# A one-core hybrid S5 and attention layer: where the side steps of the input projection stand

## The chip, the cores and the metric

The program runs on one core of a Trainium2 chip. The metric is the device time in microseconds (us). Three runs of the kernel before took 1403.91, 1406.46 and 1409.44 us; the median is 1406.46 us.

## The reference, cut to what matters

One layer works on 2048 prompt rows and 64 sample rows of width 1024. The rows are normalised and modulated, and go through one input projection with 3080 columns. Its results are split into the S5 input `u`, two gates `z`, the attention operands `q`, `k`, `v`, and eight forget logits per row.

```python
h = _rmsnorm(x, norm_g) * (1.0 + scale[:, None, :]) + shift[:, None, :]
proj = h @ w_in
u, z_s, q, k, v, z_a, f_logit = jnp.split(proj, IN_SPLITS, axis=-1)
y_ssm, h_re, h_im = _s5_segment(u, ...)        # 32 groups, 64 complex states each, a scan over time
...
logf = jax.nn.log_sigmoid((f_logit + b_f).astype(f32))
cum = jnp.cumsum(logf, axis=1)                 # the bias of the attention scores
...
y = x + gate[:, None, :] * (jnp.concatenate([y_ssm, y_att], axis=-1) @ w_out)
```

## The kernel before, in words

The program has four stages: norms of the first half of the rows, the input projection, a gated unit (GLU) with attention, and the output projection. Only the projection stage is touched by the change.

**The projection.** `InProj.line` (line 654) goes through a list of stretches. A stretch is one piece of 128 to 264 columns of `w_in` against two of the four row groups `g` (512 rows each, 576 in the last), and a stretch is cut into blocks. A block is one accumulation in one PSUM bank over the eight pieces `k` of the inner dimension, as three products per `k` (`whi` with both parts of `h`, `wlo` with the high part), 24 products in all. Each block is a generator that yields four times, every two `k`. The last two blocks of a stretch are interleaved, so that the buffers of their weights come free one after the other. Three PSUM banks (`low`) go round among the blocks; TensorE can start a block only when the bank's last content has been read out: by a copy `ev` on ScalarE for `k`, `v` and `q` (line 637), by a tanh `th` on ScalarE (L354 is the line of the helper) and a product on VectorE (L608) for `z`. The weights of the next stretch come by DMA into `wst`, ScalarE casts a high part `whi` (L319), and VectorE subtracts to `wlo` (L323).

**The side steps.** Everything else of this stage is one long generator, `side`, made by `rest()` (line 2054): the norms of the other half of the rows, the S5 set-up, 16 S5 sets, parts of the operands of the output projection, the forget logarithms, the bias of the attention and the start of the GLU. `line` takes steps from it by a share: after each block it adds the block's size times the stretch's rate (1 for `k` and `q`, 2 for `v`, 1.5 for `z`, up to 4 for `u`) to `share`, and takes that many steps (lines 688 to 691). So all of a block's steps stand behind the block's last product. TensorE's own order is the order of the program text, pinned by `Chain`. On VectorE, ScalarE and the SyncE queue (SP) a scheduler chooses the order when the program is built.

**An S5 set** (two groups of 16 channels). `consts` (line 961) builds the set's matrices in seven steps; its fifth transposes `btt` on TensorE, ScalarE copies the result to `bt` (L1010), and TensorE makes `kd` from `ca` and `bp`. `run` (line 1044) multiplies `us` by `bt` on TensorE in its first step, and then scans. `outs` (line 1102) makes the set's outputs with `tm` and `ca`. `sets` (line 1120) interleaves the steps of a set (`r`) with those of the next set's matrices (`o`):

```python
for x in "ro", "o", "r", "o", "o", "r", "o":     # line 1147: seven steps; the last "o" is the fifth of consts
    for y in x:
        next({"r": r, "o": o}[y], None)
    yield
```

The next step of `side` begins with `run` of the next set, whose product needs `bt`.

**The forget logarithms.** `logf` (line 698) stands in `rest()` behind the last S5 set. It switches ScalarE's function table (`table`, line 331), takes Abs, Exp and Ln of the logits `lf` into `lab`, finishes `lf` on VectorE (L708), switches the table back, stores `lf` to the output (L710, L711), loads it again in another order of rows (L713, L717), gives six empty steps (line 718), and then makes cumulative sums on TensorE with `triu` and `ones`. The logits of the last rows are made by the stretch `k` 1536 over the row groups 0 and 1, the fifteenth of the 24 stretches.

Of the kernel before, what the change touches and what calls it, by code (L numbers as in the profile page):

```python
# [17 lines left out]
P = 128  # L18
# [10 lines left out]
H = 8  # L29
# [419 lines left out]
class InProj:  # L449


    def __init__(self, e):
        self.e = e

        self.ht = Region(e.nc)
        self.hs = ([0, 512], [36, 512]), ([16, 640], [52, 576])
        self.dec = Region(e.nc, (70, 72), bufs=1)
        self.wp = Region(e.nc, R_WP)
        self.xp = Region(e.nc, R_X, (R_S5U[1] - 4, R_S5U[1]))
        self.ev = Region(e.nc, R_EV, bufs=2)  # L460
        self.wlo = e.V
        self.ps = Banks(e.psum, 2, 3, 4)
        self.h = {}
        self.normed = {}

    def tiles(self, g):

# [186 lines left out]
    def line(self, stretches, side, ready=None):  # L654


        w = ready
        if not w:
            w = self.fetch(*self.columns(*stretches[0][:2]))
            for _ in range(4):  # L660
                self.part(w)
        share = 0
        for j, (kind, base, row, gs, rate, after) in enumerate(stretches):
            nw = None
            bs = list(self.blocks(kind, row, gs, w))
            at = 0
            more = j + 1 < len(stretches)
            while at < len(bs):

                now = bs[at:at + (2 if more and at == len(bs) - 2 else 1)]  # L670
                for _ in range(KT // 2):
                    for _, _, b in now:
                        next(b)
                if at == 0 and more:
                    nw = self.fetch(*self.columns(*stretches[j + 1][:2]))
                at += len(now)
                with self.e.tc.high_priority():
                    if nw and at == 3:
                        self.part(nw)
                    if nw and at == len(bs):  # L680
                        while len(nw.hi) < KT:
                            self.part(nw)
                    for _, _, b in now:
                        next(b, None)
                g = now[-1][1]
                if after and (at == len(bs) or bs[at][1] != g):
                    after(g)
                share += sum(size for size, _, _ in now) * (rate[g] if isinstance(rate, dict) else rate)
                while share >= 1:
                    share -= 1  # L690
                    next(side, None)
                with self.e.tc.high_priority():
                    for _, _, b in now:
                        for _ in b:
                            pass
            w = nw

    def logf(self, ps):

        e = self.e  # L700
        nc, V, S, PL, PE = e.nc, e.V, e.S, e.PL, e.PE
        sb = self.ev
        lf = e.lf
        ab = sb.tile([P, 17, H], F32, tag="lab", name="lab", bufs=1)
        S.activation(ab, lf, AF.Abs)
        e.act(ab, ab, AF.Exp, scale=-1.0)
        e.act(ab, ab, AF.Ln, bias=1.0)
        V.scalar_tensor_tensor(lf, lf, 0.0, ab, op0=ALU.min, op1=ALU.subtract)  # L708
        lf_p, lf_s = e.o["lf_p"][0, 0], e.o["lf_s"][0, 0]
        nc.sync.dma_start(lf_p.rearrange("(f p t) h -> p f (t h)", f=2, t=TC), lf[:, :16].rearrange("p (f t) h -> p f (t h)", f=2))  # L710
        nc.sync.dma_start(e.rows(lf_s, 16), lf[:DEC, 16])  # L711

        nc.sync.dma_start(lf[:, :16], lf_p.rearrange("(t p) h -> p t h", p=P))  # L713
        cl = sb.tile([P, 5, H], F32, tag="cl", name="cl", bufs=1)
        V.memset(cl, 0.0)
        nc.sync.dma_start(cl[:, :4], e.clf.rearrange("(t p) h -> p t h", p=P))
        nc.sync.dma_start(cl[:DEC, 4], lf_s)  # L717
        for _ in range(6):
            yield
        for src, n, c0 in ((lf, 16, 0), (cl, 5, 16)):  # L720
            yield
            w = n * H
            sv = src[:, :n].rearrange("p t h -> p (t h)")
            pc = ps.tile([P, 512], F32, name="pc")
            PE.matmul(pc[:, :w], e.triu, sv, start=True, stop=True)
            pt = ps.tile([P, 512], F32, name="pt")
            PE.matmul(pt[:, :w], e.ones, sv, start=True, stop=True)
            off = sb.tile([P, 16, H], F32, tag="off", name="off", bufs=1)
            V.memset(off[:, 0], 0.0)
            yield  # L730
            for t in range(1, n):
                if t == 8:
                    yield
                V.tensor_tensor(off[:, t], off[:, t - 1], pt[:, (t - 1) * H:t * H], op=ALU.add)
            V.scalar_tensor_tensor(e.cm.rearrange("p h t -> p t h")[:, c0:c0 + n], off[:, :n], -1.0,
                                   pc[:, :w].rearrange("p (t h) -> p t h", h=H), op0=ALU.mult, op1=ALU.subtract)


class S5:
# [380 lines left out]
    def sets(self):  # L1120

        self.k, self.f = {}, {}
        self.load(0)
        o = self.consts(0)
        for _ in range(5):
            next(o)
            yield
        for s in range(NSET + 1):
            if s < NSET:
                r = self.run(s)  # L1130
                if s + 1 < NSET:
                    self.load(s + 1)
                next(r)
            if s:
                self.outs(s - 1)

            next(o, None)
            yield
            if s == NSET:
                break  # L1140
            next(r)
            next(o, None)
            yield
            next(r)
            yield
            o = self.consts(s + 1) if s + 1 < NSET else iter(())
            for x in "ro", "o", "r", "o", "o", "r", "o":
                for y in x:
                    next({"r": r, "o": o}[y], None)
                yield  # L1150
# [838 lines left out]
def body(tc, a, o):  # L1989
    with ExitStack() as top:  # L1990
# [63 lines left out]
        def rest():  # L2054
# [2 lines left out]
            yield from s5_setup  # L2057
            c = 0
            for n, _ in enumerate(s5.sets()):
                if n % 18 == 6 and c < 9:  # L2060
                    if c < 8:
                        out.raw_operands(c)
# [4 lines left out]
            assert c == 9  # L2067
            yield from s5.final()
            yield
            e.table("natural_log_exp_and_others", AF.Tanh, AF.Gelu_apprx_tanh)  # L2070
            yield from ip.logf(s5.ps)
            e.table("gelu_apprx_tanh_and_others", AF.Exp, AF.Ln, AF.Abs)
            made.append(Attn(e))
            yield
            yield from made[0].bias(s5.ps)
# [7 lines left out]
        for half in ((2, 3), (0, 1)):  # L2083
            for i, (kind, base, row) in enumerate(ip.PARTS):
                after = (lambda g: ip.get(g - 2)) if half[0] and i == 9 else None
                ts.append((kind, base, row, half, {"v": 2, "z": 1.5}.get(kind, 1), after))
        ip.line(ts, side, w)
        n = 0
# [46 lines left out]
```

## Time and profile before

| What | us |
|---|---|
| Median of the runs (lowest, highest) | 1406.46 (1403.91, 1409.44) |
| Span of the profiled execution (the page gives no other time for it) | 1410.9 |
| TensorE (PE) busy | 1318.9 |
| VectorE (DVE) busy | 972.3 |
| ScalarE (ACT) busy | 655.9 |
| GpSimd (POOL) busy | 519.8 |
| End of the projection's products, start of the GLU's | 742.9, 744.2 |

The profiled execution has a span 4.4 us above the median of the runs, and 1.5 us above the slowest of them.

In the rows below, a time stands first in microseconds from the start of the span. Of a group of instructions the page gives the line, engine, operation, what is written and read, the count, the busy time, and the idle time of the engine before them with what ended it. "PEclk" is the share of full clock that TensorE was granted. L154 is the helper line of every matrix product, L157 that of every transpose, L323 and L329 helpers of VectorE and GpSimd, so the names of the tiles tell what an instruction is.

### The profile page before, as it was taken

What the parts mean: (1) busy time and instruction counts of PE and PEld (TensorE: products, weight loads), DVE (VectorE), ACT (ScalarE), POOL (GpSimd) and SP (SyncE); (2) the same over time, 40 slices, a digit from 0 to 9 for tenths busy, and PEclk for the clock granted to TensorE, in tenths of its full rate; (3) what the DMA queues carried; (4) which work ended last, traced back from release to release, by engine and by line L of the source; (5) the groups of instructions that cost most, each with busy time, mean ns of one, the idle gap of its engine ahead of it and who ended that gap; (6) DMA issues with size and microseconds to landing.
All of it is one profiled execution on the core that took longest, in us unless ns stands there. A gap on an engine that the chain in (4) does not pass through costs nothing.

```text
span 1410.9 us, 25901 instructions
## 1 busy us (share of the span) xinstructions
PE 1318.9 (93%) x9164; PEld 1036.0 (73%) x9164; DVE 972.3 (69%) x2404; ACT 655.9 (46%) x1710; POOL 519.8 (37%) x502
## 2 busy tenths in 40 slices
PE   5898999999999899999899899999999999798998
PEld 2787999998888889898688755555555555387887
DVE  3635896987786679764326968786787786355775
ACT  3645365567443575574214435544544545522221
POOL 1100254566443446352004113423323325733453
PEclk9998999999999999999999979999999999999999
DMA  9894422534556835446239644124122123495542
GB/s 340 312 335 95 106 77 91 155 121 120 154 147 211 255 116 180 135 125 190 78 101 283 187 116 139 26 72 141 35 68 62 40 51 78 143 320 187 179 158 81
DMA packets 249476, 204.92 MB, mean 145 GB/s; under 512 B 91296, under 2 KB 217340, under 8 KB 248322
## 3 DMA queue, kind: packets, MB, share of 16 engines
q1 hardware_dynamic: 249346, 203.27, 47.0%
q8 instruction: 72, 1.18, 0.4%
q14 instruction: 58, 0.48, 0.1%
HBM read 137.68 MB, written 65.53 MB: 144 GB/s over the span
## 4 chain that ended last, share of the span: by engine, by line
PE 65%; DVE 13%; DMA 7%; issue 5%; ACT 3%; POOL 3%; SPq 3%; DVEq 0%; ACTq 0%; POOLq 0%
PE low L154 28%; PE twin L154 13%; PE bank L154 12%; PE last L154 7%; PE glu L154 2%; DMA wst<-in_w_in_dram 2%; DVE pb L1398 2%; PE bank L157 2%; DVE wlo L323 1%; POOL olb L205 1%; DMA x<-in_x_prompt_dram 1%; SPq L415 1%; PE low L157 1%; DMA lt<-t 1%; POOL qss L329 1%
## 5 line engine op out<-in xcount | busy, mean ns | idle before, releaser
L154 PE MATMUL low<-whi,h 128*128 128x256 f32 (+1 forms) x1584 | 294.6, 285 | 5.1 <-DVE th L608 4.0
L154 PE MATMUL low<-h,whi 128*128 128x256 f32 (+2 forms) x1152 | 277.3, 332 | 2.2 <-DVE th L608 1.4
L154 PEld LDWEIGHTS low<-whi,h 128*128 128x128 f32 x1584 | 248.1, 190 | 6.5 <-DVE th L608 4.2
L1398 DVE CUSTOM_DVE_ANT_0 pb<-twin,cb 128x512 bf16<-128x512 f32 (+3 forms) x328 | 200.0, 610 | 59.6 <-PE twin L154 49.8
L154 PE MATMUL low<-wlo,h 128*128 128x256 f32 (+1 forms) x816 | 229.7, 284 | 6.5 <-DVE wlo L323 6.5
L154 PEld LDWEIGHTS low<-h,whi 128*128 128x128 f32 x1152 | 197.3, 193 | 22.8 <-DVE h L323 1.9
L354 ACT ACTIVATE p<-twin 128x1024 f32<-128x1024 f32 (+3 forms) x180 | 149.8, 840 | 121.0 <-PE twin L154 110.7
L154 PE MATMUL low<-h,wlo 128*128 128x256 f32 (+2 forms) x576 | 189.4, 329 | 0.8 <-DVE wlo L323 0.8
L154 PEld LDWEIGHTS low<-wlo,h 128*128 128x128 f32 x816 | 154.8, 190 | 9.2 <-DVE wlo L323 8.8
L154 PE MATMUL bank<-p,vt 128*64 128x512 f32 (+3 forms) x704 | 143.2, 529 | 0.0
L154 PE MATMUL twin<-qs,ks 64*128 64x512 f32 (+3 forms) x1056 | 134.1, 359 | 0.0
L154 PEld LDWEIGHTS low<-h,wlo 128*128 128x128 f32 x576 | 111.4, 193 | 10.6 <-DVE wlo L323 1.9
L323 DVE TENSOR_TENSOR wlo<-wst,whi 128x512 fp32r<-128x512 f32 (+1 forms) x96 | 73.1, 767 | 66.4 <-ACT whi L319 66.1
L1476 DVE TENSOR_TENSOR acc<-acc,p 128x1024 f32<-128x1024 f32 (+4 forms) x88 | 90.1, 1024 | 30.0 <-ACT p L354 27.7
L329 POOL TENSOR_TENSOR qss<-qss,mhalf 128x4 f32<-128x4 f32 (+1 forms) x68 | 78.3, 1153 | 86.5 <-DVE qss L328 84.8
L154 PEld LDWEIGHTS twin<-qs,ks 64*128 64x128 f32 x1056 | 94.6, 190 | 11.0
L154 PE MATMUL twin<-sm,kb 64*128 64x512 f32 (+3 forms) x360 | 77.5, 426 | 22.2 <-DVE pm L1398 14.4
L154 PEld LDWEIGHTS bank<-p,vt 128*64 128x64 f32 x704 | 45.3, 140 | 64.5 <-issue 55.8
L319 ACT CAST whi<-wst 128x512 fp32r<-128x512 f32 (+1 forms) x96 | 58.8, 619 | 70.2 <-PE low L154 41.0
L205 POOL TENSOR_TENSOR x<-x,ot 128x512 f32<-128x512 f32 (+1 forms) x34 | 52.3, 1540 | 84.3 <-DVE ot L1803 79.3
L154 PEld LDWEIGHTS twin<-sm,kb 64*128 64x128 f32 x360 | 34.3, 186 | 63.0 <-DVE pm L1398 33.7
L645 ACT ACTIVATE hsq<-ev 128x64 bf16<-128x64 f32 (+1 forms) x272 | 69.8, 257 | 8.6
(437 smaller groups left out, 2641.6 us busy)
## 6 DMA issues: line engine op xcount, KB each, us to landing
wst<-in_w_in_dram SPq DMA_DIRECT2D x48, 512.0 KB
x<-in_x_prompt_dram SPq DMA_DIRECT2D x32, 512.0 KB
h<-h SPq DMA_DIRECT2D x16, 1024.0 KB
wada<-in_w_ada_dram SPq DMA_DIRECT2D x12, 1024.0 KB
cb<-cb_d SPq DMA_DIRECT2D x20, 512.0 KB
out_dram<-ev SPq DMA_DIRECT2D x64, 128.0 KB
out_dram<-x SPq DMA_DIRECT2D x32, 256.0 KB
z_d<-th SPq DMA_DIRECT2D x24, 256.0 KB
```

The source lines that it names most:

```text
L154: return self.keep(self.pe.matmul(*a, **kw))
L157: return self.keep(self.pe.transpose(*a, **kw))
L205: PL.tensor_tensor(out, x, y, op=op)
L319: i = S.copy(hi, x)
L323: V.tensor_tensor(lo, x, hi, op=ALU.subtract)
L329: PL.tensor_tensor(out, out, bc(mhalf[:out.shape[0]], list(out.shape)), op=ALU.pow)
L354: i = S.activation(out, x, func, **kw)
L415: x = nc.sync.dma_start(w[:, 4 * k2:4 * k2 + 4], e.w_ada[512 * k2:512 * k2 + 512, n * 512:n * 512 + 512] .rearrange("(k p) c -> p k c", p=P))
L645: S.activation(sq[:r], tv[:, h], AF.Square, accum_out=ss[:r, h:h + 1])
L1398: V.tensor_tensor_reduce(b[:, :n], ps[:, h, :n], cb[:, h, :n], 1.0, NEG, ALU.add, ALU.max, accum_out=self.pm[:, t, h, pi:pi + 1])
L1476: (PL if j else V).tensor_tensor(y[:rows, :, c0:nq], x[:rows, :, c0:nq], p[:rows, :, :n], op=ALU.add)
```

## The change

It has three parts.

1. A block's share of side steps is added in four quarters, after every two `k`, and steps are taken inside the block as soon as the share reaches one. The steps per block stay the same in number. At rate 1 nothing changes except in the interleaved pair of blocks, which has two steps: one now comes in the middle.
2. In `sets`, the last two `r` and `o` steps move one place forward and an empty step ends the seven. So one more step lies between the transposes of a set's `btt` and the products that use `bt`.
3. `logf` is cut in two. `logs` holds the table switches, the logarithms, the stores and the loads; it is called once, at a step number ending in 5, as soon as the logits of all rows are there (`forget` is set by the stretch `k` 1536 of the row groups 0 and 1). The cumulative sums stay at their place behind the last set. The six empty steps go and one is added.

```diff
@@ line
-                for _ in range(KT // 2):
+                g = now[-1][1]
+                each = sum(size for size, _, _ in now) * (rate[g] if isinstance(rate, dict) else rate) / (KT // 2)
+                for k in range(KT // 2):
                     for _, _, b in now:
                         next(b)
+                    share += each
+                    if k < KT // 2 - 1:
+                        share = self.aside(side, share)
...
-                share += sum(size for size, _, _ in now) * (rate[g] if isinstance(rate, dict) else rate)
-                while share >= 1:
-                    share -= 1
-                    next(side, None)
+                share = self.aside(side, share)
...
+    @staticmethod
+    def aside(side, share):
+
+        while share >= 1:
+            share -= 1
+            next(side, None)
+        return share
+
+    def logs(self):
+
+        e = self.e
+        nc, V, S, sb, lf = e.nc, e.V, e.S, self.ev, e.lf
+        e.table("natural_log_exp_and_others", AF.Tanh, AF.Gelu_apprx_tanh)
         ab = sb.tile([P, 17, H], F32, tag="lab", name="lab", bufs=1)
-        S.activation(ab, lf, AF.Abs)
+        e.act(ab, lf, AF.Abs)
         e.act(ab, ab, AF.Exp, scale=-1.0)
         e.act(ab, ab, AF.Ln, bias=1.0)
+        e.table("gelu_apprx_tanh_and_others", AF.Exp, AF.Ln, AF.Abs)
         V.scalar_tensor_tensor(lf, lf, 0.0, ab, op0=ALU.min, op1=ALU.subtract)
...
         nc.sync.dma_start(cl[:DEC, 4], lf_s)
-        for _ in range(6):
-            yield
-        for src, n, c0 in ((lf, 16, 0), (cl, 5, 16)):
+
+    def logf(self, ps):
+
+        e = self.e
+        V, PE, sb = e.V, e.PE, self.ev
+        for src, n, c0 in ((e.lf, 16, 0), (self.cl, 5, 16)):
             yield
...
@@ sets
-            for x in "ro", "o", "r", "o", "o", "r", "o":
+            for x in "ro", "o", "r", "o", "ro", "o", "":
...
@@ rest
             for n, _ in enumerate(s5.sets()):
+                if n % 10 == 5 and ip.forget == 1:
+                    ip.forget = n
+                    ip.logs()
+                    yield
...
-            e.table("natural_log_exp_and_others", AF.Tanh, AF.Gelu_apprx_tanh)
             yield from ip.logf(s5.ps)
-            e.table("gelu_apprx_tanh_and_others", AF.Exp, AF.Ln, AF.Abs)
...
@@ body
+                if not half[0] and not i:
+                    after = lambda g: setattr(ip, "forget", g)
```

Three places of the built order show what moves. The first is TensorE at the fifteenth S5 set. `low` and `bank` are PSUM banks; rows with `whi` or `wlo` are the projection's. Before:

```order
L154 MATMUL low_132<-whi_1_192,h_53248_1_382 128x256
L157 MATMUL low_144<-ident_0_82,btt_0_2779 128x128 x2
L154 MATMUL bank_77<-ca_0_2787,bp_0_2784 32x128 x2
L154 MATMUL bank_81<-us_2_3050,bt_0_2821 128x264
L154 MATMUL low_124<-us_2_3050,bt_0_2821 128x264
L154 MATMUL low_128<-us_1_2825,tm_1_3111 128x264
```

And now:

```order
L157 MATMUL low_144<-ident_0_82,btt_0_2765 128x128 x2
L154 MATMUL bank_77<-ca_0_2787,bp_0_2784 32x128 x2
L154 MATMUL low_140<-whi_1_192,h_16384_1_381 128x256
L154 MATMUL low_140<-wlo_1_193,h_16384_1_381 128x256
L154 MATMUL low_140<-whi_1_192,h_53248_1_382 128x256
...
L154 MATMUL low_136<-whi_0_188,h_36864_0_285 128x256
L154 MATMUL bank_81<-us_2_3050,bt_0_2807 128x264
L154 MATMUL low_124<-us_2_3050,bt_0_2807 128x264
```

Here 36 rows of projection products now stand between the transposes of `btt` and the products with `bt`, where none stood. Over the 16 sets, ten had none before; now every set has at least 12 rows of them.

The second place is the SP queue around the forget logarithms: `lf` is stored to the output (`out_dram`) and loaded again. Before, among the stores of the last `z` gates:

```order
L609 DMA z_d<-th_1_1606 128x2x256
L710 DMA out_dram<-lf_0_118 128x2x64
L711 DMA out_dram<-lf_0_118 8x8x8
L713 DMA lf_0_118<-out_dram 128x16x8
L717 DMA cl_0_7680<-out_dram 64x8
L609 DMA z_d<-th_0_1529 128x2x256
```

And now, among the stores of `k` (`ev`), with the next load of weights (`wst`) some rows behind:

```order
L653 DMA out_dram<-ev_0_537 128x256
L720 DMA out_dram<-lf_0_118 128x2x64
L721 DMA out_dram<-lf_0_118 8x8x8
L723 DMA lf_0_118<-out_dram 128x16x8
L727 DMA cl_0_5760<-out_dram 64x8
L653 DMA out_dram<-ev_1_564 128x256
L653 DMA out_dram<-ev_2_595 128x256
```

The round trip stands some 140 rows earlier in this queue, and the sums on TensorE that read it stand where they stood, within 50 rows.

The third place is TensorE in the early `u` stretches, where a step is four transposes of `x` for the norm. A piece of the difference, with what goes to the middle of a block:

```order
 L154 MATMUL low_132<-h_53248_1_382,whi_0_188 128x256
 L154 MATMUL low_132<-h_16384_1_381,wlo_0_189 128x256
+L157 MATMUL low_124<-ident_0_82,x_0_145 128x128
+L157 MATMUL low_124<-ident_0_82,x_1_147 128x128
+L157 MATMUL low_124<-ident_0_82,x_0_145 128x128
+L157 MATMUL low_124<-ident_0_82,x_1_147 128x128
 L154 MATMUL low_132<-h_16384_1_381,whi_1_192 128x256
 L154 MATMUL low_132<-h_53248_1_382,whi_1_192 128x256
```

So one group of transposes moves 12 products forward there. Behind the projection, TensorE's order is the same in both programs.

More of the change, by code (lines that the diff above doesn't have):

```diff
@@ L464, in __init__ @@
         self.normed = {}
+        self.forget = -1
     def tiles(self, g):
@@ L684, in line @@
                         next(b, None)
-                g = now[-1][1]
                 if after and (at == len(bs) or bs[at][1] != g):
                     after(g)
-                share += sum(size for size, _, _ in now) * (rate[g] if isinstance(rate, dict) else rate)
-                while share >= 1:
-                    share -= 1
-                    next(side, None)
+                share = self.aside(side, share)
                 with self.e.tc.high_priority():
@@ L696, in line @@
             w = nw
-    def logf(self, ps):
+    @staticmethod
[5 more added lines that the diff above has]
+    def logs(self):
         e = self.e
-        nc, V, S, PL, PE = e.nc, e.V, e.S, e.PL, e.PE
-        sb = self.ev
-        lf = e.lf
+        nc, V, S, sb, lf = e.nc, e.V, e.S, self.ev, e.lf
+        e.table("natural_log_exp_and_others", AF.Tanh, AF.Gelu_apprx_tanh)
         ab = sb.tile([P, 17, H], F32, tag="lab", name="lab", bufs=1)
-        S.activation(ab, lf, AF.Abs)
+        e.act(ab, lf, AF.Abs)
         e.act(ab, ab, AF.Exp, scale=-1.0)
         e.act(ab, ab, AF.Ln, bias=1.0)
+        e.table("gelu_apprx_tanh_and_others", AF.Exp, AF.Ln, AF.Abs)
         V.scalar_tensor_tensor(lf, lf, 0.0, ab, op0=ALU.min, op1=ALU.subtract)
@@ L713, in logf @@
         nc.sync.dma_start(lf[:, :16], lf_p.rearrange("(t p) h -> p t h", p=P))
-        cl = sb.tile([P, 5, H], F32, tag="cl", name="cl", bufs=1)
+        cl = self.cl = sb.tile([P, 5, H], F32, tag="cl", name="cl", bufs=1)
         V.memset(cl, 0.0)
```

## The prediction, as it was put on record

> **What bounds the kernel now.** I read the page first, then the busy time by stage, and then, inside the projection, what TensorE waited for.
>
> ```profile
> span 1410.9 us, 25901 instructions
> PE 1318.9 (93%) x9164; PEld 1036.0 (73%) x9164; DVE 972.3 (69%) x2404; ACT 655.9 (46%) x1710; POOL 519.8 (37%) x502
> 150.00:350.00 200.00, 192.11 (x1510) 185.37 (x1509) 168.73 (x537) 117.76 (x490) 105.73 (x123) 1.00 0.39 114
> 450.00:660.00 210.00, 199.72 (x1452) 188.45 (x1452) 143.80 (x379) 121.93 (x482) 91.19 (x119) 0.97 0.54 168
> ```
>
> TensorE is busy 93% of the span. In the last two rows (stretch, its length, then busy PE, weight loads, DVE, ACT, POOL, granted clock, DMA share, GB/s) it is busy 96% and 95%, while VectorE reaches 84% at most. TensorE is the bound, it works strictly in the program's order, and what the change can give is TensorE's idle time and the time it runs at a lower clock. The waits of TensorE from 100 to 660 us (total, times, longest):
>
> ```profile
> PE low L154 <- DVE wlo L323: 7.3, 13, 1.5
> PE low L154 <- DVE th L608: 5.4, 2, 4.0
> PE low L154 <- ACT bt L1010: 4.9, 8, 1.8
> PE bank L154 <- ACT bt L1010: 2.9, 3, 1.8
> PE low L157 <- ACT hf L521: 2.6, 3, 1.6
> ```
>
> Rows three and four are the wait that the free step aims at: 7.8 us in 11 waits. The second view is of the stretches around the longest gaps, in the columns named above.
>
> ```profile
> 122.00:132.00 10.00, 7.44 (x38) 6.88 (x38) 4.41 (x9) 5.21 (x11) 0.00 (x0) 0.66 0.91 195
> 134.00:144.00 10.00, 8.33 (x58) 7.80 (x58) 4.35 (x16) 4.70 (x13) 0.54 (x1) 0.83 0.07 26
> 470.00:482.00 12.00, 8.04 (x45) 7.83 (x44) 9.40 (x22) 6.57 (x32) 9.25 (x12) 0.72 0.95 322
> 496.00:502.00 6.00, 4.92 (x16) 4.01 (x17) 4.34 (x16) 5.28 (x23) 1.19 (x2) 0.72 0.44 126
> 584.00:590.00 6.00, 4.19 (x13) 3.33 (x12) 4.06 (x16) 2.80 (x7) 0.55 (x3) 0.72 0.56 165
> 669.00:675.70 6.70, 0.86 (x4) 0.40 (x3) 1.23 (x2) 1.10 (x2) 0.38 (x1) 0.92 0.54 125
> 675.70:682.00 6.30, 6.29 (x18) 5.14 (x19) 2.89 (x17) 0.00 (x0) 0.00 (x0) 0.54 0.06 20
> ```
>
> Each gap is paid twice: once as idle time, and once more in the microseconds behind it, where the clock is down. I price the second part as (1 - granted clock) times PE's busy time. For the last gap this is 0.46 x 6.29 = 2.9 us.
>
> **The logarithms taken earlier.** The chain of waits (start, length, what) shows the longest gap of the projection whole:
>
> ```profile
> 665.85 1.28 ACT L334
> 668.23 1.31 DVE lf L708
> 669.56 2.85 DMA out_dram<-lf
> 672.43 3.14 DMA lf<-out_dram
> 675.71 0.77 PE low L154 x2
> ```
>
> Two DMA trips through HBM stand between the logarithm and the sums, and TensorE has run dry: 6.70 - 0.86 = 5.8 us idle, with 2.9 us at the lower clock behind it, 8.7 us. In the changed order the trips are issued some 150 us before the sums, so the gap goes whole: **-8.7 us**. The two table loads (1.28 us by the row), three short functions and four DMAs move to about 500 us.
>
> ```profile
> 495.00:515.00 20.00, 18.19 (x130) 17.01 (x128) 16.69 (x47) 15.12 (x71) 10.57 (x15) 0.91 0.35 102
> ```
>
> ScalarE has 4.9 of 20 us free there, and the loads take 2 x 1.28 = 2.6. Cover: the three PSUM banks. Without it, 2.6 us come back. On this the Trainium skill speaks against the change: "ScalarE: Activation LUTs", section "What ACT_TABLE_LOAD costs", puts a switch at 2.66 us with its drain, so 5.3 us for two, which would be over the free time by 0.4 us. The row here shows 1.28 us and the next function 0.01 us behind it, so the trace does not show that drain. On SP the load must wait for the store to land: 672.43 - 669.56, some 2.9 us in which the queue stands. Behind it wait stores of `k` from a ring of four buffers, four blocks long, and the next weights, needed a stretch later; I cost this at nothing. VectorE also waits at `lf` for the last logarithm, in front of S5 work; the smallest lead of that work over TensorE is 9.2 us (below), so nothing again. If either cover fails, a gap like the one removed comes back: 8.7 us.
>
> **The free step.** The fifteenth set, on TensorE (start, length, tile, and in brackets the idle time before it) and then on ScalarE:
>
> ```profile
> 583.30 0.38 PE L157 MATMUL low<-ident,btt 128*128 128x128 f32 x2
> 583.62 0.41 PE L154 MATMUL bank<-ca,bp 128*32 128x128 f32 x4
> 585.83 1.18 PE L154 MATMUL bank<-us,bt 128*128 128x264 f32 x2 [1.81 <-ACT bt L1010]
> 584.89 0.62 ACT L319 CAST whi<-wst 128x512 fp32r<-128x512 f32 x1 [0.97 <-DMA wst<-in_w_in_dram]
> 585.42 0.37 ACT L1010 COPY bt<-low 128x256 f32<-128x256 f32 x1
> ```
>
> `bt` needs only a copy of 0.37 us, but that stands behind a weight cast that waits for a DMA. Now every set has at least 12 projection products in between. Their time comes from this pair of rows:
>
> ```profile
> 116.11 0.40 PE L154 MATMUL low<-h,whi 128*128 128x256 f32 x2
> 116.47 0.40 PE L154 MATMUL low<-h,whi 128*128 128x256 f32 x2
> ```
>
> Three products (two here, a third between) take 0.36 us, so 12 take 1.4 us, and the 36 of this set 4.3 us. The sets with long waits have 24 products (2.8 us) or more, and no wait was over 1.81 us. So the 7.8 us of idle time go. With them go the lowered clocks behind 497 and 585 us: 0.28 x 4.92 + 0.28 x 4.19 = 2.6 us. I take off 0.8 us because at 585 us the cast itself was late, and TensorE meets it soon after. **-9.6 us**; bounds -7 (idle time alone, less this) and -10.4. The Trainium skill would take less: "TensorE: Matmul & The Clock Gate", section "What's actually happening", halves the clock after an idle window of some 3.4 us, and these gaps last 1.8 us, so by it the 2.6 us need not go and the sum would be 2.6 us smaller. The trace shows the clock at 0.72 behind both gaps, so I follow the rows.
>
> The transposes come one step earlier, so `ca` and `btt` must be ready earlier. VectorE's last `ca` and the transposes that follow it:
>
> ```profile
> 535.90 0.99 DVE L989 TENSOR_TENSOR ca<-ca,lin 128x288 f32<-128x288 f32 x1
> 546.12 0.38 PE L157 MATMUL low<-ident,btt 128*128 128x128 f32 x2
> ```
>
> The last `ca` is done at 536.89, 9.2 us ahead, the smallest slack I found; a step here is one block, 2.8 us. No new wait.
>
> **Steps inside the blocks.** In the early stretches five groups of transposes stood in a row with two banks to go round, and TensorE waited three times for the copy `hf`; a later one waited for the sample rows:
>
> ```profile
> 121.06 1.03 PE L157 MATMUL low<-ident,x 128*128 128x128 f32 x8
> 125.96 1.11 PE L157 MATMUL low<-ident,x 128*128 128x128 f32 x4 [1.62 <-ACT hf L521]
> 137.07 0.43 PE L157 MATMUL low<-ident,x 64*128 64x64 f32 x4 [1.67 <-issue]
> ```
>
> Idle and clock of the two stretches: 2.56 + 0.34 x 7.44 and 1.67 + 0.17 x 8.33, 8.2 us. Now 12 products stand between most groups. But `hf` still stands behind a cast that waits for weights, and the order of the set-up's loads has changed, so I take half: **-4 us**, bounds 0 and -8.2.
>
> At 470 us TensorE waited 3.96 us for the read-out of a `z` block, which had waited for its buffer while the DMA share was 0.95: 3.96 + 0.28 x 8.04 = 6.2 us. In the new order ScalarE reads this bank only after the copy of the second `k` block, so a copy, a tanh and VectorE's product are waited for again, some 1.4 us and perhaps the clock. **-2 us**, bounds 0 and -6.2.
>
> Against this: at two boundaries of stretches the last weight splits now stand behind 17 rows of S5 work on VectorE, where 3 stood. The same rows before, first and last:
>
> ```profile
> 463.16 0.42 DVE L1071 TENSOR_TENSOR w<-bank,co 128x256 f32<-128x256 f32 x1 [0.75 <-ACT pr L1065]
> 468.73 0.85 DVE L1084 TENSOR_TENSOR_SCAN zs<-r,zs,ws 128x8 f32<-128x8 f32 x2
> ```
>
> They last about 6 us. The S5 products now stand in the middle of the interleaved pair. From there the split is done after about 1.4 (first product and its copies) + 6 + 0.7 = 8.1 us. TensorE needs it after the S5 products (2.5), the second half of the pair (2.8) and 12 to 18 products (1.4 to 2.1), 6.7 to 7.4 us. So it waits some 1 us at each, with 1.3 us of clock behind it: **+4 us**, bounds 0 and, with the longest VectorE wait seen (3.96) at both, +10.
>
> The sum is -8.7 - 9.6 - 4 - 2 + 4 = -20.3 us against the span of 1410.9, which stands 4.4 us over the median of the runs. The same difference from the median, 1406.46, gives 1386; I say **1387**, since removed gaps seldom go without a rest. All other instructions stay, and behind the projection nothing moves.
>
> **The rivals.** *Half of it stays* (chance 0.22): TensorE arrives earlier and meets the next late thing, weights or splits, so that the free step gives its small waits alone. For it speaks that casts wait for `wst` around 495 and 585 us; against it, that all `wlo` waits together were 7.3 us. Log gap -8.7, half of 7.8, nothing else, and +2: 1396. *No change* (0.08): the log gap is replaced by one of the same size at 500 us (the standing queue), and the early gaps and the new splits cancel the rest: about 1403. *Slower* (0.08): the splits. Where VectorE is 84% busy, S5 work handed out in the middle of the pair stands ahead of the weights of the next stretch at every one of the 14 boundaries, not at two. At 2.5 us (between 1 and 3.96) and 1.3 us of clock each this decides from the seventh boundary on; at nine, 1406.5 - 24.3 + 9 x 3.8 = 1416. Against it, the printed order has the long run of rows at two boundaries only.
>
> **How the numbers follow.** My forecast has 0.62, with its own range 1377 to 1395: all of the early and the 470 us gaps gone at one end, the splits at +10 and half of the clock term kept at the other. The whole range must reach to the first rival: 1377 to 1402. A measurement of this kernel tells about 0.5% from no change, so faster is below 1399.4: 0.62 and most of the first rival, 0.78. Within 0.5%: 0.14. Slower: 0.08.
>
> **What would show it.** In the changed profile: no wait of TensorE for `lf`, clock 1.0 around the sums; the waits for `bt` under 1 us in all; the clock between 122 and 144 us above 0.9; waits for `wlo` near 9 us. It is wrong if `bt` is still waited for, if the waits for `wlo` or `th` grow by over 10 us, or if a gap appears at 500 us.

## The result and the profile after

The changed kernel took 1392.24 us (median of four runs, 1391.25 to 1393.9), the kernel before 1407.95 us beside it. The ratio is 0.9899, with a 95% interval of 0.9877 to 0.9922: 15.7 us faster by the medians, between 11 and 17 by the interval. The forecast was 1387 us with a range of 1377 to 1402, so the sign and the range held, and the gain was 4 us smaller than forecast. The profiled execution of the change has a span of 1391.4 us, 19.5 us under that of before. In the runs on record a span is 1.6 to 2.0 us shorter than the time of the same execution. The profiled execution of the change is the one of 1393.23 us, 1.0 us above its median. That of before has no time on record; with 1.6 us added to its span it took some 1412.5 us (an estimate), 4.6 us above its median here and longer than any of the 49 timed executions of that kernel, of which the longest took 1411.45 us. So the two profiled executions lie further apart than the medians.

The page of the changed kernel, its first lines:

```profile
span 1391.4 us, 25886 instructions
PE 1312.5 (94%) x9164; PEld 1031.9 (74%) x9164; DVE 968.5 (70%) x2404; ACT 652.0 (47%) x1710; POOL 520.5 (37%) x502
```

Where the time went shows best in five stretches from 75 us to the end of the projection. The columns are the stretch, its length, busy PE, weight loads, DVE, ACT, POOL, granted clock, DMA share and GB/s. First the kernel before:

```profile
75.00:150.00 75.00, 66.42 (x507) 60.25 (x507) 35.88 (x99) 40.48 (x89) 5.41 (x9) 0.93 0.61 183
150.00:450.00 300.00, 288.65 (x2066) 269.63 (x2065) 248.21 (x717) 161.84 (x621) 150.13 (x185) 1.00 0.43 127
450.00:490.00 40.00, 36.04 (x256) 35.06 (x256) 23.86 (x64) 19.55 (x78) 13.57 (x19) 0.91 0.90 308
490.00:600.00 110.00, 103.68 (x787) 98.31 (x786) 89.01 (x224) 67.01 (x254) 55.11 (x77) 0.97 0.47 140
600.00:745.00 145.00, 137.74 (x755) 117.95 (x754) 57.56 (x149) 58.47 (x191) 29.78 (x33) 0.98 0.40 122
```

And the changed kernel:

```profile
75.00:150.00 75.00, 65.30 (x503) 58.73 (x502) 36.76 (x102) 40.55 (x88) 5.85 (x9) 0.95 0.61 179
150.00:450.00 300.00, 291.49 (x2091) 272.36 (x2090) 247.95 (x716) 161.71 (x623) 150.50 (x185) 1.00 0.45 132
450.00:490.00 40.00, 35.31 (x257) 34.03 (x256) 26.88 (x72) 21.03 (x87) 16.21 (x23) 0.96 0.83 270
490.00:600.00 110.00, 107.87 (x848) 103.62 (x847) 89.64 (x229) 70.98 (x278) 55.90 (x78) 1.00 0.51 152
600.00:745.00 145.00, 143.34 (x822) 123.61 (x820) 63.45 (x159) 58.83 (x177) 32.29 (x33) 1.00 0.48 152
```

Idle time is the length less the busy PE, and clock loss is (1 - clock) times busy PE, as in the forecast. Their sum over the five rows was 51.2 us before and is 31.4 us now, 19.8 us less, which is the difference of the two spans within 0.3 us. (The last row of the changed kernel holds some 20 us of the GLU as well, since its projection ends earlier: the first product of the GLU stands at 725.0 us, where it stood at 744.2. The gain is all made by then.)

| Stretch, us | idle + clock before | now | difference |
|---|---|---|---|
| 75 to 150 | 8.6 + 4.6 | 9.7 + 3.3 | -0.2 |
| 150 to 450 | 11.4 + 0 | 8.5 + 0 | -2.8 |
| 450 to 490 | 4.0 + 3.2 | 4.7 + 1.4 | -1.1 |
| 490 to 600 | 6.3 + 3.1 | 2.1 + 0 | -7.3 |
| 600 to 745 | 7.3 + 2.8 | 1.7 + 0 | -8.4 |

So nearly all of the gain is behind 490 us, and nothing in the early stretch, where the forecast had put 4 us. The changed kernel was profiled a second time among the experiments. By the same reckoning the last two stretches have 2.2 and 1.4 us of idle time and clock loss there, as in the first profile. Its first and third stretch are worse:

```profile
75.00:150.00 75.00, 63.42 (x477) 56.52 (x476) 34.85 (x88) 38.13 (x84) 5.85 (x9) 0.93 0.60 177
450.00:490.00 40.00, 36.52 (x257) 34.93 (x256) 25.18 (x65) 18.32 (x74) 14.42 (x21) 0.91 0.92 313
```

That is 16.0 us from 75 to 150 us, where the kernel before had 13.2, and 6.8 us from 450 to 490 us. So the gain behind 490 us repeats, and the smaller differences ahead of it are no firmer than one execution.

The waits of TensorE from 60 to 735 us in the changed kernel, first profile (total, times, longest; rows that nothing below rests on are left out):

```profile
PE low L154 <- DVE wlo L323: 7.1, 12, 1.4
PE low L154 <- DVE th L609: 3.5, 1, 3.5
PE low L157 <- DVE x L496: 3.2, 2, 1.8
PE low L157 <- DVE ss L328: 3.1, 1, 3.1
PE low L154 <- ACT bt L1023: 1.6, 2, 0.9
PE low L154 <- DMA h<-h: 1.2, 1, 1.2
PE low L154 <- ACT ev L638: 0.9, 1, 0.9
```

The wait for `lf` is gone, and the sums start with no idle time ahead of them (the first row below, TensorE). The waits for `bt` fell from 7.8 to 1.6 us, those for weight splits `wlo` stayed (7.3 before), and the wait for `th` at 470 us is 3.5 us where it was 4.0. Two new waits came, for the reload of `h` and for the copy `ev`. And the early transposes wait longer for the rows `x` and for `ss`, the sums that the norm needs: 6.3 us, where the kernel before had 1.3 and 1.5.

```profile
647.99 0.38 PE L154 MATMUL low<-lf,triu 128*128 128x128 f32 x2
513.41 0.39 PE L154 MATMUL low<-whi,h 128*128 128x256 f32 x1 [0.87 <-ACT ev L638]
```

The second row is the price of the logarithms at their new place: both profiles of the changed kernel have this wait (0.87 and 1.05 us), and the kernel with the logarithms back at their old place, below, has none there. ScalarE's rows there, the two table loads and the function behind each:

```profile
497.48 1.28 ACT L334 ACT_TABLE_LOAD   x1
498.78 0.32 ACT L354 ACTIVATE lab<-lf 128x136 f32<-128x136 f32 x1
...
500.65 1.28 ACT L334 ACT_TABLE_LOAD   x1
501.95 0.26 ACT L646 ACTIVATE hsq<-ev 128x64 bf16<-128x64 f32 x1
```

The next function starts 0.02 us behind each load. The cover held all but 0.9 us.

### The profile page after: what moved, and what is told of

It reads as the page before. It is cut to its first block, busy times and chain, and to the rows that moved or that the text cites. A ratio compares the mean times of both kernels' runs of the same rounds, so it can differ in the third digit from the quotient of the medians.

```text
span 1391.4 us, 25886 instructions
## 1 busy us (share of the span) xinstructions
PE 1312.5 (94%) x9164; PEld 1031.9 (74%) x9164; DVE 968.5 (70%) x2404; ACT 652.0 (47%) x1710; POOL 520.5 (37%) x502
## 4 chain that ended last, share of the span: by engine, by line
PE 63%; DVE 11%; DMA 6%; POOL 4%; issue 4%; ACT 3%; SPq 1%; DVEq 0%; ACTq 0%; POOLq 0%
PE low L154 25%; PE twin L154 13%; PE bank L154 12%; PE last L154 7%; PE glu L154 3%; DVE pb L1411 2%; PE bank L157 2%; DMA wst<-in_w_in_dram 1%; POOL qss L329 1%; POOL olb L205 1%; DMA lt<-t 1%; DVE acc L1489 1%; ACT p L354 1%; DVE ev L650 1%; DVE wlo L323 1%
```

## The experiments

Each kernel was timed in five rounds beside the kernel before on the same chip. Three chips were used, on which the kernel before had a median of 1407.45 us (the first four kernels), 1405.75 us (the next four) and 1408.14 us (the last four), so ratios are what is compared between them.

### Each part alone, and two together

The logarithms early and nothing else. The edit to the kernel before:

```diff
+                if n % 10 == 5 and ip.forget == 1:
+                    ip.forget = n
+                    ip.logs()
+                    yield
```

(with `logf` cut in two and `forget` set, as in the change).

> The kernel before with the third part of the change alone: the logarithms taken between S5 sets at about 500 us, old step order in the sets, steps behind the blocks. Separate gaps (my theory): the wait of TensorE for lf (5.8 us) and the lowered clock behind it (2.9 us) both go, no new gap at 500 us: 8 to 9 us faster, about 1399.5. Gap moved (rival): the table loads and the standing SP queue make a like gap near 500 us: within 2 us of the kernel before.

1397.59 us, ratio 0.9927 (0.9914 to 0.994): 10 us faster. The expectation held, and the gap did not move to 500 us: from 490 to 600 us TensorE's clock is 1.00, and its idle time is 4.0 us, where the kernel before had 6.3. Not all of the 10 us is the gap, though. The early call takes a step of its own, which shifts the later sets against the blocks, and the waits for `bt` fell as well, from 7.8 to 5.5 us.

The free step and nothing else:

```diff
-            for x in "ro", "o", "r", "o", "o", "r", "o":
+            for x in "ro", "o", "r", "o", "ro", "o", "":
```

> The kernel before with the free step in the sets alone. Separate gaps: the waits for bt fall from 7.8 us to under 2 us and the clock behind 497 and 585 us is whole, 7 to 9 us faster, about 1400. Late thing next (rival): TensorE only meets the late cast or split sooner, waits for wlo, th or ev grow by what the waits for bt lose, 3 to 4 us faster, about 1404. Needs the other part (second rival): without steps inside the blocks some sets still have no projection products between the transposes and the products with bt, and half of the waits stay, 4 us faster.

1404.75 us, ratio 0.9977 (0.9966 to 0.9989): 2.7 us saved where 7 to 9 were expected. TensorE's waits for `bt` in it:

```profile
PE bank L154 <- ACT bt L1010: 2.9, 2, 1.9
...
PE low L154 <- ACT bt L1010: 1.5, 3, 0.9
```

4.4 us of the 7.8 stayed. The printed order of TensorE says why. I counted, for each of the 16 sets, the projection products between the transposes of `btt` and the first product with `bt`:

| Kernel | sets with none | with under 12 | waits for `bt`, us |
|---|---|---|---|
| before | 11 | 11 | 7.8 |
| logarithms alone | 7 | 7 | 5.5 |
| free step alone | 4 | 4 | 4.4 |
| steps inside the blocks alone | 0 | 2 | 4.5 |
| the change | 0 | 0 | 1.6 |

(The text ahead of the prediction says ten sets without products before; counted like this there are eleven.) A free step is a step only when steps are taken one at a time. Behind a block at rate 2, or behind an interleaved pair, two to six steps are taken at once, and an empty one among them puts no product in between. So the second rival of the expectation was right: this part needs the first. What it does save ahead of the sums is in part lost there: the wait for `lf` is 6.7 us in its trace, where it was 5.8.

Steps inside the blocks and nothing else:

```diff
+                    share += each
+                    if k < KT // 2 - 1:
+                        share = self.aside(side, share)
...
-                share += sum(size for size, _, _ in now) * (rate[g] if isinstance(rate, dict) else rate)
-                while share >= 1:
-                    share -= 1
-                    next(side, None)
+                share = self.aside(side, share)
```

> The kernel before with steps inside the blocks alone. By the prediction's terms (-4 early, -2 at 470 us, +4 for the splits) 2 us faster. By the profile of the changed kernel, whose lead at 146 us is 0.3 us, its waits for wlo the same and its wait for th 0.5 us shorter: no change, within 2 us of the kernel before. Hidden carrier (rival): the steps inside the blocks carry most of the gain, by moving the waits for bt behind products, 6 us or more faster.

1399.63 us, ratio 0.9937 (0.9922 to 0.9952): 7.8 us faster, where the prediction's terms gave 2. The rival that I held unlikely was right in the time, but not in the way it gave: the waits for `bt` fell only from 7.8 to 4.5 us. Above all this part removes the gap at the logarithms, which are at their old place in this kernel. ScalarE's table loads, then TensorE's sums:

```profile
648.65 1.28 ACT L334 ACT_TABLE_LOAD   x1
...
650.63 1.28 ACT L334 ACT_TABLE_LOAD   x1
```

```profile
663.94 0.38 PE L154 MATMUL low<-lf,triu 128*128 128x128 f32 x2
```

From the first load to the sums there are 15.3 us here, and TensorE is not idle ahead of them. Before, the load stood at 665.85, and TensorE was ready for the sums at 669.9 already (675.7 less its 5.8 us of idle time), 4 us later. The six empty steps are the same in both. But in the kernel before, five of the steps are taken at one time behind an interleaved pair, so only two blocks lie between; with the steps spread over the quarters of the blocks, the same six mean four times as much time.

The logarithms and the free step together, the steps behind the blocks as before (of the change's edits the one in `line` undone):

```diff
-                    share += each
-                    if k < KT // 2 - 1:
-                        share = self.aside(side, share)
...
-                share = self.aside(side, share)
+                share += sum(size for size, _, _ in now) * (rate[g] if isinstance(rate, dict) else rate)
+                while share >= 1:
+                    share -= 1
+                    next(side, None)
```

> The changed kernel without its first part: steps behind the blocks, the free step and the early logarithms kept. Separate gaps: as fast as the changed kernel within 2 us, about 1392 (the gains of the two parts add up). Steps inside cost time (rival): 4 us faster than the changed kernel, about 1388. Steps inside carry it (rival): 5 us or more slower than the changed kernel, about 1398.

1400.99 us, ratio 0.9951 (0.9937 to 0.9965): 7 us behind the changed kernel by the ratios, and 3.4 us slower than the logarithms alone, the intervals of these two just meeting. The last rival was right. Its longest new wait, and the two rows that lead to it, on TensorE, ScalarE and VectorE:

```profile
565.11 2.13 PE L154 MATMUL bank<-us,bt 128*128 128x264 f32 x4 [4.98 <-ACT bt L1022]
```

```profile
564.32 0.19 ACT L1130 COPY rot<-co 128x2 f32<-128x2 f32 x1 [3.54 <-DVE co L1005]
564.42 0.36 ACT L638 COPY ev<-low 128x256 f32<-128x256 f32 x1
564.68 0.38 ACT L1022 COPY bt<-low 128x256 f32<-128x256 f32 x1
```

The same set in the kernel with the logarithms alone, ScalarE and then TensorE:

```profile
564.61 0.38 ACT L1022 COPY bt<-low 128x256 f32<-128x256 f32 x1
```

```profile
565.04 1.16 PE L154 MATMUL bank<-us,bt 128*128 128x264 f32 x4 [0.63 <-ACT bt L1022]
```

`bt` is copied at the same moment in both, since the copy stands on ScalarE behind `rot`, which waits for VectorE's `co`. TensorE came to it some 4.3 us earlier and waited there. This is the forecast's first rival, "TensorE arrives earlier and meets the next late thing", at one place.

### The change with one part undone

Without the free step (the `sets` line as before):

```diff
-            for x in "ro", "o", "r", "o", "ro", "o", "":
+            for x in "ro", "o", "r", "o", "o", "r", "o":
```

> The changed kernel without the free step (old order of the steps in the sets). Free step still earns its waits for bt (theory): the kernel with the steps inside the blocks alone waits 4.5 us for bt and the changed one 1.6 us, so this one is 3 to 5 us slower than the changed kernel, 1395 to 1397. Free step costs (rival): with the logarithms early it made that pair 3.4 us slower, because the transposes come sooner than what they need; then this one is about 3 us faster than the changed kernel, 1389.

1399.73 us, ratio 0.9957 (0.9942 to 0.9972): 8 us behind the changed kernel by the ratios, so the free step earns, more than the 3 to 5 us expected. Its trace does not show the reason that I gave. The waits for `bt` come to 2.8 us, 1.2 more than in the changed kernel. The larger loss stands behind the early logarithms:

```profile
514.98 0.58 PE L154 MATMUL low<-whi,h 128*128 128x256 f32 x1 [2.69 <-ACT ev L638]
```

```profile
490.00:600.00 110.00, 106.81 (x818) 102.79 (x817) 89.00 (x226) 69.61 (x270) 54.05 (x77) 0.97 0.49 147
```

The wait for `ev` is 2.7 us where the change has 0.9, and the clock is 0.97 over the stretch, where the change has 1.00: 0.03 x 106.8 = 3.2 us. Together with `bt` that is some 6 us, but the trace as a whole does not lose so much: its span is 1394.5 us, 3.1 us over that of the change, for the profiled execution was the fastest of six (1396.27 to 1403.11 us). What the slower ones lose is not shown. This kernel is also 4 us slower than the logarithms alone, with the intervals just apart, so beside the early logarithms neither of the other two parts earns anything without the other.

Without the early logarithms (at their old place, with the six empty steps):

```diff
-                if n % 10 == 5 and ip.forget == 1:
-                    ip.forget = n
-                    ip.logs()
-                    yield
...
+            ip.logs()
+            for _ in range(6):
+                yield
             yield from ip.logf(s5.ps)
```

> The changed kernel with the logarithms back at their old place behind the last set, with six empty steps. Shared gap (theory): the steps inside the blocks spread those empty steps over more products, so the gap at the sums is gone without the early logarithms: within 2 us of the changed kernel, about 1392. Early logarithms earn 9 us whatever stands beside them (rival): 1401.

1390.61 us, ratio 0.9893 (0.988 to 0.9905), against 0.9899 for the change: no difference beyond the intervals. The expectation held, and the sums start without idle time in its trace:

```profile
655.97 0.38 PE L154 MATMUL low<-lf,triu 128*128 128x128 f32 x2
```

The part that is worth 10 us alone is worth nothing measurable beside the other two, since the steps inside the blocks remove the same gap.

Without the steps inside the blocks of the `u` stretches:

```diff
-                    if k < KT // 2 - 1:
+                    if k < KT // 2 - 1 and kind != "u":
```

> The changed kernel with the steps of the u stretches (to about 150 us) taken behind the blocks again, everything else kept. Steps inside the early blocks cost time (theory): the two kernels with them lose 0.7 and 3.9 us on TensorE between 72 and 146 us and the three without them -1.1 to 1.0, so this one is about 2 us faster than the changed kernel, 1390. As predicted (rival): they win 4 us, 1396. Neither (rival): the differences there are the weather of the first loads, 1392.

1388.77 us, ratio 0.9886 (0.9869 to 0.9903). It was run again beside the changed kernel itself:

> The changed kernel once more, for comparison on the same chip with the three that follow: 14 to 16 us faster than the kernel before, ratio 0.989 to 0.990.

> Again the changed kernel with the steps of the u stretches behind the blocks. Steps inside the early blocks cost time (theory): 2 us faster than the changed kernel in the same call. Weather of the loads (rival): within 1 us of it.

The change had 1392.74 us there (0.9897, 0.9878 to 0.9916), and the variant 1390.15 us (0.9879, 0.9859 to 0.99). It was 2 us faster both times by the ratios, and the intervals overlap both times, so the size is likely but not settled. What the traces show is the place. The first groups of transposes in the kernel before, and the same in the changed one:

```profile
87.73 0.33 PE L157 MATMUL low<-ident,x 128*128 128x128 f32 x1 [1.31 <-DVE x L495]
89.59 0.98 PE L157 MATMUL low<-ident,x 128*128 128x128 f32 x7 [1.53 <-DVE ss L328]
```

```profile
87.33 0.33 PE L157 MATMUL low<-ident,x 128*128 128x128 f32 x1 [3.12 <-DVE ss L328]
89.07 0.90 PE L157 MATMUL low<-ident,x 128*128 128x128 f32 x3 [1.41 <-DVE x L496]
```

The transposes stand 12 products further ahead (some 1.4 us), and they start only 0.4 and 0.5 us sooner, since `ss` and `x` come little earlier. So TensorE waits 4.5 us in place of 2.8. This repeats in every trace of this case: the two waits come to 3.9 to 4.6 us in the five traces with the steps inside these blocks, and to 2.8 us in all nine without.

Both of the last two edits at once:

> Both at once: the logarithms at their old place with six empty steps, and the u stretches' steps behind the blocks; the free step and the steps inside the later blocks stay. Shared gap (theory): the early logarithms earn nothing beside the steps inside the blocks, and the u stretches' part costs 2 us, so 2 us faster than the changed kernel, 17 us faster than the one before. Rival: the early logarithms earn their gap: 8 us slower than the changed kernel.

1389.91 us, ratio 0.9878 (0.9856 to 0.99). This agrees with both readings, and it does without the early logarithms; it is not clearly faster than the change either.

### The distance to the sums, by itself

The kernel before with ten empty steps for six:

```diff
-        for _ in range(6):
+        for _ in range(10):
             yield
```

> The kernel before with ten empty steps ahead of the sums in place of six, and nothing else. Distance (theory): of the six steps most are taken at one time behind the interleaved pair, so they stand for two blocks only; four more add at least one block of 5.6 us, the gap of 5.8 us and the clock behind it go, 8 us faster, about 1399.5. Place (rival): the logarithms wait for ScalarE's tanh and casts there, and the gap stays or moves, within 3 us of the kernel before.

1403.36 us, ratio 0.9985 (0.9973 to 0.9998): 2.4 us faster, as the rival had it, though the gap is gone from its trace, as the theory had it. Its last stretch:

```profile
600.00:745.00 145.00, 141.53 (x806) 122.24 (x805) 60.77 (x149) 60.56 (x187) 30.68 (x32) 1.00 0.45 138
```

Idle and clock loss are 3.5 us there, where the kernel before had 10.1, so this one execution saves 6.6 us. A new wait of 2.1 us, for `cm` behind the sums, is part of the 3.5:

```profile
685.19 0.44 PE L157 MATMUL low<-ident,cm 128*128 128x128 f32 x2 [2.06 <-DVE cm L735]
```

The profiles flatter this kernel. Its profiled execution is the fastest of its twelve timed ones (1400.84 to 1408.05 us), 2.5 us under their median, and that of before stood above its median. What the slower executions lose, and so why the gain is 2.4 us and not 6.6, is not shown. The logarithms alone remove the same gap and gain 10 us. Two differences are on record: that kernel has no wait for `cm`, and its waits for `bt` are 5.5 us, where they are 8.2 here. How much of the 10 us is the gap alone is therefore open.

This kernel has the program of the kernel before up to 640 us, and so it shows what is fixed and what is not. The same wait for `bt`, before and here:

```profile
497.08 2.05 PE L154 MATMUL low<-us,bt 128*128 128x264 f32 x4 [1.81 <-ACT bt L1010]
```

```profile
495.73 1.16 PE L154 MATMUL low<-us,bt 128*128 128x264 f32 x4 [1.69 <-ACT bt L1010]
```

The gap is there both times. But the four products behind it last 2.05 us in one and 1.16 us in the other: the clock fell once and not the other time. The same holds at the fifteenth set (gaps of 1.81 and 1.56 us): the clock fell there in the kernel before and not here. From 490 to 600 us the granted clock was 0.97 in the kernel before and 1.00 here, with like idle time.

### The wait at 470 us

The kernel with the `u` stretches' steps behind the blocks, and the 256-wide pieces of `z` in the ring of four small buffers:

```diff
-        if kind == "u" and n == 256:
+        if n == 256:
             x = self.ev.tile([P, 256], F32, tag="ev", name="ue", bufs=4)
```

> The kernel with the u stretches' steps behind the blocks, and the 256-wide pieces of z read into the ring of four small buffers in place of the two large ones. The wait at 470 us is for a buffer (theory): its idle time of 3.3 us and the clock behind it go, 3 to 5 us faster than without this edit. The busy DMA (rival): h is loaded again at that time, the small ring's own stores are as late, and the wait stays under another name, within 1 us.

1396.05 us, ratio 0.9918 (0.9892 to 0.9944): not faster, and by the medians 6 us slower than without this edit on the same chip, where the intervals just overlap. Neither expectation held in the time. The wait for `th` is gone, and this stands in its place on TensorE:

```profile
477.04 0.59 PE L154 MATMUL low<-whi,h 128*128 128x264 f32 x1 [4.58 <-DMA h<-h]
479.63 0.81 PE L154 MATMUL low<-whi,h 128*128 128x264 f32 x2 [1.79 <-DMA h<-h]
```

Without this edit, in the second of the two runs of that kernel, the same two places read:

```profile
467.86 0.39 PE L154 MATMUL low<-whi,h 128*128 128x264 f32 x1 [3.60 <-DVE th L609]
479.36 0.54 PE L154 MATMUL low<-whi,h 128*128 128x264 f32 x2 [3.44 <-DMA h<-h]
```

In the first of them it waited 3.27 and 0.53 us there. So 6.4 us of waiting with the edit stand against 7.0 and 3.8 us without: the wait for `h` differs that much from one execution to the next. The rows for `h` (DMAs of 1 MB) come at their own time, and a TensorE that isn't held up for `th` waits for them. Why the median is 6 us longer is not shown; the profiled execution took 1394.59 us, only 2.7 us more than the one whose rows stand above.

## Why the prediction was right, and where not

The time came out inside the range and on the side that was forecast. That the sum was near is luck in part, though: two terms were put down to the wrong part, one gain was not made, and one cost was not paid. Of the signs that the prediction named, the wait for `lf` is gone, the clock is 1.00 over the last stretch and 0.92 from 122 to 144 us, and no gap of the old size stands at 500 us. The waits for `bt` (1.6 us) did not fall under 1 us, and those for `wlo` (7.1 us) did not grow to 9.

- **The logarithms, -8.7.** The gap was sized rightly in the traces: from 600 to 745 us the change saved 8.4 us, the idle time is gone, and the early logarithms cost 0.9 us of waiting for `ev`. The 10 us (8 to 12) of this part alone hold more than the gap. What failed is the silent step that only this part can remove it. "The gap goes whole" is as true of the steps inside the blocks, because six empty steps mean little time where five of them are taken at once. So the change's parts, which alone give 10, 2.7 and 7.8 us, give 15.7 together.
- **The table loads.** "The trace does not show that drain": the changed trace agrees, with 0.02 us between load and function. The drain that the Trainium skill states in "ScalarE: Activation LUTs", section "What ACT_TABLE_LOAD costs", would have cost two more pauses there; the rows show none behind either load.
- **The free step, -9.6.** In the whole change the waits for `bt` fell to 1.6 us, as the step said but for a rest. But it is not this part's own: alone it gave 2.7 us, and beside the logarithms alone it lost 3.4 us, with the intervals just meeting. "Now every set has at least 12 projection products in between" is true only with steps inside the blocks.
- **The clock behind the gaps of 1.8 us, 2.6 of the 9.6.** This term failed. I took one execution's clock for a fixed price. In two of the three kernels whose rows at the first of these places are compared here (the logarithms alone: 1.16 us for the four products behind 1.67 us of idle time; ten empty steps: 1.16 us behind 1.69) the clock stayed up. In the kernel with ten empty steps it stayed up at the second place too. "I follow the rows" was right to follow measurement, but one row is one draw. The Trainium skill, in "TensorE: Matmul & The Clock Gate", section "What's actually happening", says that the clock falls after at least one idle window of some 3.4 us, that the window runs freely and does not begin with the kernel, and that the count of slow products at a kernel's start varies from run to run. The fall behind the 1.81 us gap of before goes against the length of the window; that the outcome varies agrees, here in mid-kernel. By its rule the sum would have been 2.6 us smaller, and so the forecast 1389.6, nearer to the 1392.24 measured.
- **Steps in the early blocks, -4.** Wrong. From 75 to 150 us the change saved 0.2 us in its first profile and lost 2.8 us in its second; the variant without these steps was 2 us faster twice, not clear of the interval. The waits for `hf` did ease, as the step said: 2.6 us before, none in the first profile of the change and 1.3 us in the second. The step that failed left out that other transposes come sooner to an `x` that is hardly earlier: the waits for `x` and `ss` rose from 2.8 to 6.3 us. The wait of 1.67 us that the prediction puts down to the sample rows has "issue" in its row, which means that the profile shows nothing it waited for; it was 1.1 and 1.8 us in the change.
- **The 470 us gap, -2.** The stretch from 450 to 490 us gave 1.1 us in the first profile, all of it clock: its idle time grew by 0.7. In the second it gave 0.4. The wait for `th` went from 4.0 to 3.5 us and one of 1.2 us for `h` came behind it. With the buffer out of the way TensorE waits for `h`, of which the DMA share of 0.90 in that row could have warned; the step that failed saw only the buffer.
- **The weight splits, +4.** Not paid: 7.1 us of waits for `wlo` where there were 7.3. The long run of S5 rows ahead of the splits exists in VectorE's order, but TensorE still found them done. The rival *slower*, which rested on it, has nothing for it.
- **The rival *half stays*.** Its mechanism is real and was seen at 565 us in the kernel without steps inside the blocks (4.98 us of waiting for a copy that was no later than elsewhere). In the full change it decided little.

Against the profile of before the sum was nearly exact, -20.3 us forecast and -19.8 us in the table above, by luck, because two misses cancel: early -4 forecast and -0.2 found, splits +4 forecast and nothing paid. What it missed is the step "the same difference from the median". The difference of the medians is 15.7 us, 3.8 less than that of the two profiled executions. Every term was read from one execution that stood some 4.6 us above its median, and part of what it showed, the 2.6 us of clock, the other execution with the same rows doesn't have. The profiled execution of the change stood 1.0 us above its own median. What makes up the rest of the 3.8 us is not shown.

## What to carry to other kernels

A slack that is counted in steps is worth what lies between two steps: look at how many are taken at one time before counting on an empty one. Two parts of a change that remove the same gap don't add, so ask of each gap which of the parts could remove it alone. And price only idle time as sure; a lowered clock behind a gap of 1.6 to 3.5 us differed here from one execution to the next, and belongs in the range.

## What was not expected of the hardware

The same gap of TensorE, 1.7 to 1.8 us in front of one set's products with `bt`, was followed by four products of 2.05 us in one kernel and of 1.16 us in two others, which have the same order on TensorE up to there. At 470 us a gap of 3.49 us and one of 3.48 us, in two executions of the changed kernel, left the clock at 0.96 and 0.91 over the stretch from 450 to 490 us. And in the kernel with the steps inside the blocks alone the clock stayed whole behind a gap hardly shorter:

```profile
475.27 0.39 PE L154 MATMUL low<-whi,h 128*128 128x264 f32 x1 [3.36 <-DVE th L608]
...
450.00:490.00 40.00, 34.32 (x258) 32.81 (x257) 25.18 (x63) 18.20 (x71) 15.41 (x22) 1.00 0.93 320
```

The long gap at the sums, which the free step alone left in place, had a lowered clock behind it both times it was traced: 0.98 over the last stretch in the kernel before, and 0.96 there:

```profile
670.99 0.77 PE L154 MATMUL low<-lf,triu 128*128 128x128 f32 x2 [6.67 <-DMA lf<-out_dram]
...
600.00:745.00 145.00, 136.92 (x748) 117.20 (x747) 56.15 (x143) 57.13 (x180) 26.40 (x29) 0.96 0.41 124
```
